# Softmax weights left unscaled until a head pair is mixed; the reciprocal sums travel through DRAM

## The chip, the core and the metric

The kernel runs on one core of a Trainium2 chip. The core has TensorE (PE in the profile, with its weight loader PEld), VectorE (DVE), ScalarE (ACT), GpSimd (POOL) and SyncE (SP), which issues most of the DMAs. The metric is the device time of one execution in microseconds (us). All arithmetic is float32; products are made in the float32r format from a high and a low part of each operand, so most data exist as two tiles, `hi` and `lo`.

## The reference

Two layers on 512 frames of 1024 channels. The first mixes by pooling, the second by attention; each ends in a gated MLP. What the change touches is the attention of the second layer, with 16 heads of 64 channels; for 512 frames its band is causal by chunks of 64 and covers all earlier chunks.

```python
q = head_rmsnorm(q.reshape(B, S, N_HEADS, HEAD_DIM), q_norm)
k = head_rmsnorm(k.reshape(B, S, N_HEADS, HEAD_DIM), k_norm)
...
    s = jnp.einsum('bqhd,bkhd->bhqk', qc, kb).astype(jnp.float32) * scale + bias[None]
    s = jnp.where(valid[None, None, None, :], s, -1e30)
    p = jax.nn.softmax(s, axis=-1).astype(vb.dtype)
    return jnp.einsum('bhqk,bkhd->bqhd', p, vb)
...
return o @ w_o
```

## The kernel before

The residual stream X is kept channel-major: 8 tiles of 128 channels by 512 frames. The attention first projects and forms the values V (`opening`), then runs a loop over 64 tiles: 16 heads, and for each head 4 tiles `t` of 128 query frames, tile `t` seeing `(t+1)*128` keys. Two heads make a pair `p`, and a pair's result is one tile O2 of 128 channels (64 of each head) by 512 frames.

One step of the loop works on several tiles at once, shifted by `LAG` = 2 and `LAGM` = 2 steps:

- `scores(h, t)`: PE makes the scores of a tile in PSUM (`sc`, L1394 and L1395). DVE adds the bias B and writes the tile `sb` with its row minimum (L1398). ACT takes the exponential and its row sum (L1400). DVE takes the reciprocal of the sum (L1401), and ACT multiplies the tile by it (L1402). At a head's first tile two DMAs on SP load its bias from DRAM (L1389).
- `turn(h, t)`, two steps later: PE transposes the tile in blocks of 128x128 (`tp`, L1410), and ACT and DVE split it into high and low parts (`pt0h`, `pt0l` for even heads, `pt1h`, `pt1l` for odd ones; by the helper `split`, L102 and L103).
- `mix(h)`, two steps after a head's last `turn`: PE multiplies V with the transposed tiles (`oo`, L1422); the products with V's high and low part lie in different halves of the partitions, so ACT copies one (`ob`, L1427) and DVE adds the other into the pair's O2 (`o`, L1428).
- `channel_major(p, i)`: PE transposes queries and keys of the next pair (`zt`), POOL and SP's DMAs bring them into the forms that `scores` reads (`z`, `zh`).

PE's order is written by hand (`manual_schedule`); between the steps `fill` puts PE work in proportion: the last part of the second projection, the third and fourth, and from step 35.5 on the output projection `outputs` (tiles `wo`). This needs O2 split into high and low parts (`two<-o` in the profile, L102 and L103), which is written once a pair is done and its room is free. The output projection takes pairs 0 to 3, then 4 and 5; pairs 6 and 7 (`wo_6`) come after the loop. X is added by DVE (L1348).

On the other engines, and on SP, the order in the loop is made by a scheduler that simulates the program when it is built. Each engine runs its own rows strictly in that order, and a row that waits holds all rows behind it. POOL splits the weights of the projections (L103), and up to pair 5 also both parts of the output weights (L100 and L103).

Of the kernel before, what the change touches and what calls it, by code (L numbers as in the profile page):

```python
# [17 lines left out]
F32 = mybir.dt.float32  # L18
F32R = mybir.dt.float32r
AF = mybir.ActivationFunctionType  # L20
# [3 lines left out]
P = 128  # L24
S = 512
# [5 lines left out]
HD = 64  # L31
NPAIR = H // 2
TT = S // P
# [39 lines left out]
def trunk(ctx: ExitStack, tc: tile.TileContext, xt, xT, cols, band, edge, poolw, gv, wout, wqk, wv, wo, rel, out):  # L73
    nc = tc.nc
# [3 lines left out]
    tmp = ctx.enter_context(tc.tile_pool(name="tmp", bufs=1))  # L78
    dram = ctx.enter_context(tc.tile_pool(name="dram", bufs=1, space=bass.MemoryType.DRAM))
# [9 lines left out]
    def psum(tag, name, bufs=2):  # L89
        return ps.tile([P, S], F32, name=name, tag=tag, bufs=bufs)  # L90
# [3 lines left out]
    def g_tile(name):  # L94
        return tmp.tile([P, S], F32, name=name, tag="g", bufs=6)
# [45 lines left out]
    def small(name, n, tag="nw"):  # L141
        return tmp.tile([P, n], F32, name=name, tag=f"{tag}{n}", bufs=4)
# [213 lines left out]
    ones = consts.tile([P, 1], F32, name="ones")  # L356
    gq = consts.tile([P, 2], F32, name="gq")
    rdram = dram.tile([H, RLEN], F32, name="rdram")
    ET = mybir.EngineType
    with tc.tile_pool(name="start", bufs=1) as sp, tc.manual_schedule(engines={ET.PE, ET.DVE, ET.Activation, ET.Pool, ET.SP}):  # L360
        first, second, acc0 = mixer(sp)

    def ffn(l, first, pool, acc, summed=None, upool=None, hook=None):
# [56 lines left out]
        def early():  # L420
# [6 lines left out]
            for at, (f, k, i) in enumerate(units):  # L427
# [13 lines left out]
                if at == (19, 14)[l]:  # L441

                    order = tc.manual_schedule(engines={ET.DVE, ET.Activation}) if l == 0 else nullcontext()
                    order.__enter__()
# [388 lines left out]
        def tour():  # L833
# [8 lines left out]
            def place(f, k):  # L842

                for word in PLACES[k].split():
                    x, name = word.split(".")
                    step = steps_of(f + "qofn".index(x) - 2).get(name)
                    if step:
                        step()

            for f in range(KIND.index("s"), NF + 2):  # L850
# [10 lines left out]
                for k in range(7):  # L861
                    if (f, k) == (ORDERED, 0):
                        order.enter_context(tc.manual_schedule(engines={ET.DVE, ET.Activation, ET.SP}))
                    place(f, k)
# [50 lines left out]
    def attention(rest, hook, hidden_slots):  # L915
        XS = set2
        O2, V, Z, QK, SM = {}, {}, {}, {}, {}
# [463 lines left out]
        def scores(h, t):  # L1381

            p, e = divmod(h, 2)
            q, k, kl = QK[p, 0][e], QK[p, 1][e], KL[p % 2][e]
            if t == 0:

                base = rdram[h, :]
                for r, n in ((0, S - HD), (HD, S)):
                    nc.sync.dma_start(BT[h % 2][r:r + HD, S - n:], bass.AP(tensor=base.tensor, offset=base.offset + HD, ap=[[1, HD], [1, n]]))  # L1389
            n = (t + 1) * P  # L1390
            nw = max(n, 256)

            sc = psum("S", f"sc{h}_{t}", 4)
            nc.tensor.matmul(sc[:, :nw], q[:, t * P:n], k[:, :nw], start=True, stop=False)  # L1394
            nc.tensor.matmul(sc[:, :nw], q[:, t * P:n], kl[:, :nw], start=False, stop=True)  # L1395
            SM[h, t] = s_ = heads.tile([P, n], F32, name=f"sb{h}_{t}", tag=f"sb{t}")
            mx = tmp.tile([P, 3], F32, name=f"mx{h}_{t}", tag="mx", bufs=4)
            nc.vector.tensor_tensor_reduce(out=s_[:, :n], in0=sc[:, :n], in1=BT[h % 2][:, :n][:, ::-1], scale=1.0,  # L1398
                                           scalar=3e38, op0=OP.add, op1=OP.min, accum_out=mx[:, 0:1])
            nc.scalar.activation(s_[:, :n], s_[:, :n], AF.Exp, scale=-1.0, bias=mx[:, 0:1], accum_out=mx[:, 1:2])  # L1400
            nc.vector.reciprocal(mx[:, 2:3], mx[:, 1:2])  # L1401
            nc.scalar.activation(s_[:, :n], s_[:, :n], AF.Copy, scale=mx[:, 2:3])  # L1402

        def turn(h, t):

# [7 lines left out]
        def mix(h):  # L1413

            p, e = divmod(h, 2)
            hs = slice(e * HD, (e + 1) * HD)
            oo = psum("S", f"oo{h}", 4)
            if p not in O2:
                O2[p] = heads.tile([P, S], F32, name=f"o2_{p}", tag="o2", bufs=4)
            for c in range(2):  # L1420
                for j in range(TT):
                    nc.tensor.matmul(oo[:, j * P:], V[j, h // 4][:, h % 4].rearrange("p a d -> p (a d)"),  # L1422
                                     PT[e][c][:, 4 * j:3 * j + TT].rearrange("p t q -> p (t q)"),
                                     start=j == 0 and c == 0, stop=j == TT - 1 and c == 1)
            ob = g_tile(f"ob{h}")
            other = slice(HD - e * HD, 2 * HD - e * HD)
            nc.scalar.activation(ob[hs], oo[other], AF.Copy)  # L1427
            nc.vector.tensor_add(O2[p][hs], oo[hs], ob[hs])  # L1428

        r2, late = small("r2", TT), []  # L1430
        closing = ExitStack()
        with tc.tile_pool(name="pre", bufs=1, reuse_waits="tile") as pre:
            with tc.manual_schedule(engines={ET.PE, ET.DVE, ET.Activation, ET.SP}):
                rcol, second = opening(pre)
        heads = closing.enter_context(tc.tile_pool(name="bh", bufs=1, reuse_waits="tile"))
# [9 lines left out]
        with tc.manual_schedule(engines={mybir.EngineType.PE}):  # L1445
# [17 lines left out]
            for i in range(nb + LAG + LAGM):  # L1463
                steps = []
                if i < nb:
                    steps.append(lambda: scores(*tiles_[i]))
                if i % 8 in CM and i // 8 + 1 < NPAIR:
                    steps.append(lambda: channel_major(i // 8 + 1, CM.index(i % 8)))
                j = i - LAG
                if 0 <= j < nb:  # L1470
                    steps.append(lambda: turn(*tiles_[j]))
                j2 = j - LAGM
                if 0 <= j2 < nb and j2 % TT == TT - 1:
                    steps.append(lambda: mix(tiles_[j2][0]))
                for x, step in enumerate(steps):
                    step()
                    if late and x < 2:
                        late.pop(0)()
                    fill(i + (x + 1) / len(steps))

                while 8 * kept + 7 <= j2 and (cur == 3 or cur == 2 and done >= 24 * (kept // 2 + 1)):
                    split(O2[kept], XS[kept], XS[KD + kept])
                    kept += 1
# [41 lines left out]
    with tc.tile_pool(name="ba", bufs=1, reuse_waits="tile") as big:  # L1525
        rest = attention(rest, hook, hidden_slots)
# [55 lines left out]
```

## Time and profile before

| | |
|---|---|
| runs, median (lowest to highest) | 966.68 us (966.43 to 966.88) |
| profiled execution, its own time | 969.2 us |
| its span, first to last instruction | 967.4 us |
| head loop in it | about 440 to 605 us |
| ACT busy / DVE busy, whole span | 594.0 us / 849.5 us |
| DMA, mean over the span | 107 GB/s |

A page names an engine, the line of the kernel, the operation and its tiles (`out<-in`); a helper's line, such as L103, stands for many callers, so tiles tell them apart. PE's matmuls are pipelined, so "busy" is not the same as working at full pace; the time from one start to the next shows the pace. A row's idle time in brackets is that of the engine just before it, with what ended it.

### The profile page before, as it was taken

Reading aid. Unit: us, or ns where it says so; the run is one execution under the profiler, and the core shown is the slowest. Engines: PE = TensorE matmul, PEld = TensorE weight load, DVE = VectorE, ACT = ScalarE, POOL = GpSimd, SP = SyncE. Lnnn points to the kernel's source line nnn. Section 1 sums busy time; section 2 is a strip of 40 time slices with the busy share of each in tenths; the row PEclk is TensorE's granted clock in tenths of the full one; section 3 lists DMA queues with packets and bytes.
Section 4 is the critical chain, followed back from the end, with each engine's and each line's share of the span. In section 5 each row is a group of like instructions: output and inputs, shape, how many; then the busy total and the mean of one; then the engine's idle time right before and its main releaser. Section 6 shows DMA issues by size and latency. Waiting matters only on the chain.

```text
span 967.4 us, 13737 instructions
## 1 busy us (share of the span) xinstructions
PE 956.3 (99%) x4958; PEld 810.0 (84%) x4958; DVE 849.5 (88%) x1522; ACT 594.0 (61%) x1023; POOL 91.2 (9%) x81
## 2 busy tenths in 40 slices
PE   8999999999999999999999999999999999999998
PEld 7788988888888888888888777888988888888886
DVE  8999999999899859895786887999999999989953
ACT  7665554655555457466898888656565565456531
POOL 2300000000000000043525441000000000000000
PEclk9999999999999999999999999999999999999999
DMA  9222332332323317024433341332333233332323
GB/s 343 73 97 71 115 108 81 120 120 80 114 79 120 102 48 292 21 66 133 132 113 97 88 117 55 100 109 80 94 115 108 84 120 111 102 104 79 114 79 111
DMA packets 38996, 103.87 MB, mean 107 GB/s; under 512 B 4464, under 2 KB 7936, under 8 KB 38928
## 3 DMA queue, kind: packets, MB, share of 16 engines
q1 hardware_dynamic: 38864, 102.95, 33.0%
q8 instruction: 39, 0.64, 0.3%
q14 instruction: 29, 0.24, 0.1%
q0 software_dynamic: 32, 0.04, 0.0%
q10 hardware_dynamic: 32, 0.00, 0.0%
HBM read 96.65 MB, written 2.14 MB: 102 GB/s over the span
## 4 chain that ended last, share of the span: by engine, by line
PE 87%; DVE 8%; ACT 2%; DMA 1%; issue 1%; SPq 0%; POOL 0%; DVEq 0%; ACTq 0%; POOLq 0%
PE st_m L593 10%; PE out L124 8%; PE out L125 8%; PE out L123 8%; PE st_m L595 5%; PE st_t L593 5%; PE gv L124 4%; PE gv L125 4%; PE gv L123 4%; PE qk L123 3%; PE qk L124 3%; PE qk L125 3%; PE st_t L595 3%; PE st_b L593 3%; PE tp L1410 1%; PE st_b L595 1%
## 5 line engine op out<-in xcount | busy, mean ns | idle before, releaser
L124 PE MATMUL out<-one,ow_h 128*128 128x512 f32 x224 | 88.1, 393 | 0.0
L123 PE MATMUL out<-one,ow_h 128*128 128x512 f32 x224 | 88.0, 393 | 0.0
L125 PE MATMUL out<-one,ow_l 128*128 128x512 f32 x224 | 87.9, 393 | 0.0
L829 DVE TENSOR_TENSOR X<-out,X 128x512 f32<-128x512 f32 (+1 forms) x65 | 44.3, 683 | 45.9 <-PE out L125 45.6
L593 PE MATMUL st_m<-two,g_h 128*128 128x512 f32 x240 | 75.1, 394 | 0.1
L593 PE MATMUL st_m<-h,g_h 128*128 128x512 f32 x240 | 74.1, 390 | 0.0
L392 ACT ACTIVATE ow_h<-wo_r 128x768 fp32r<-128x768 f32 (+1 forms) x56 | 44.4, 794 | 43.4 <-PE out L124 39.8
L407 DVE SCALAR_TENSOR_TENSOR c<-a,col,c 128x511 f32<-128x511 f32 (+1 forms) x76 | 56.8, 749 | 0.0
L593 PEld LDWEIGHTS st_m<-h,g_h 128*128 128x128 f32 x240 | 45.1, 188 | 10.3
L595 PEld LDWEIGHTS st_m<-two,g_l 128*128 128x128 f32 x240 | 45.0, 188 | 9.6
L593 PEld LDWEIGHTS st_m<-two,g_h 128*128 128x128 f32 x240 | 44.0, 188 | 10.4 <-ACT w L602 0.8
L393 DVE TENSOR_TENSOR ow_l<-wo_r,ow_h 128x768 fp32r<-128x768 f32 (+1 forms) x56 | 50.4, 899 | 2.3 <-ACT ow_h L392 2.3
L602 ACT ACTIVATE w<-st_m 128x512 f32<-128x512 f32 x30 | 18.0, 598 | 55.2 <-PE st_m L595 55.2
L595 PE MATMUL st_m<-h,g_l 128*128 128x256 f32 x240 | 48.3, 283 | 0.0
L595 PE MATMUL st_m<-two,g_l 128*128 128x256 f32 x240 | 47.6, 280 | 0.0
L124 PEld LDWEIGHTS out<-one,ow_h 128*128 128x128 f32 x224 | 42.4, 189 | 5.7 <-DVE one L418 0.3
L125 PEld LDWEIGHTS out<-one,ow_l 128*128 128x128 f32 x224 | 42.4, 189 | 5.5
L123 PEld LDWEIGHTS out<-one,ow_h 128*128 128x128 f32 x224 | 42.4, 189 | 5.4
L1398 DVE CUSTOM_DVE_ANT_0 sb<-sc,B 128x128 f32<-128x128 f32 (+1 forms) x64 | 31.1, 486 | 17.9 <-PE sc L1395 13.3
L404 ACT ACTIVATE c<-a,col 128x512 f32<-128x512 f32 x38 | 30.7, 813 | 23.8 <-DVE a L751 22.2
L392 ACT ACTIVATE g_h<-gv_r 128x1024 fp32r<-128x1024 f32 x32 | 33.7, 1055 | 13.5 <-DMA gv_r<-gv 12.9
L1400 ACT ACTIVATE sb<-sb,mx 128x128 f32<-128x128 f32 (+1 forms) x64 | 35.7, 558 | 9.8 <-DVE mx L1398 9.2
(459 smaller groups left out, 3035.7 us busy)
## 6 DMA issues: line engine op xcount, KB each, us to landing
gv_r<-gv SPq DMA_DIRECT2D x86, 512.0 KB, 3.9
wo_r<-wout SPq DMA_DIRECT2D x32, 384.0 KB, 3.1
wo_r<-wout SPq DMA_DIRECT2D x32, 320.0 KB, 2.9
wqk_r<-wqk SPq DMA_DIRECT2D x12, 512.0 KB, 3.5
b<-wv SPq DMA_DIRECT2D x8, 512.0 KB, 6.7
wo_r<-wo SPq DMA_DIRECT2D x8, 512.0 KB, 3.6
xt<-xt SPq DMA_DIRECT2D x4, 512.0 KB, 5.2
X<-xT SPq DMA_DIRECT2D x8, 256.0 KB, 7.5
```

The costliest lines, as they stand in the source:

```text
L123: yield nc.tensor.matmul(o, sh, mh, start=first, stop=False, **how)
L124: yield nc.tensor.matmul(o, sh, ml, start=False, stop=False, **how)
L125: yield nc.tensor.matmul(o, sl, mh, start=False, stop=last, **how)
L392: nc.scalar.activation(hi[:, :n], raw[:, :n], AF.Copy)
L393: return hi, lo, lambda: nc.vector.tensor_sub(lo[:, :n], raw[:, :n], hi[:, :n].bitcast(F32))
L404: nc.scalar.activation(c, a, AF.Identity, scale=cw[2], bias=cw[3])
L407: nc.vector.scalar_tensor_tensor(c[:, j:], a[:, :S - j], cw[2 - j], c[:, j:], op0=OP.mult, op1=OP.add)
L593: nc.tensor.matmul(o, hi[:, c], B[i, name], start=first and i == 0, stop=False, **how)
L595: nc.tensor.matmul(o[:, 0], lo[:, c], B[i, name][:, 0], start=False, stop=i == 3, **how)
L829: nc.vector.tensor_add(X[d][:, fs], o[:, fs], X[d][:, fs])
L1398: nc.vector.tensor_tensor_reduce(out=s_[:, :n], in0=sc[:, :n], in1=BT[h % 2][:, :n][:, ::-1], scale=1.0, scalar=3e38, op0=OP.add, op1=OP.m ...
L1400: nc.scalar.activation(s_[:, :n], s_[:, :n], AF.Exp, scale=-1.0, bias=mx[:, 0:1], accum_out=mx[:, 1:2])
```

## The change

The tile of exponentials is not multiplied by the reciprocal of its sum any more. It is transposed, split and mixed as it is. The 8 sums of a pair (2 heads by 4 tiles, 128 query frames each) are collected in one tile `sums`, 128 partitions by 8. After the last exponential of a pair one DVE reciprocal gives `rr`; a DMA on SP writes it to DRAM turned around (`rinv`, 8 rows of 128 floats), and two more read it back, 512 floats of a head spread over that head's 64 partitions (`rb`). When the pair is mixed, one multiplication of O2 by `rb` puts the scale in: on POOL for pairs 0 to 6, on DVE for the last. `rb` has one buffer; O2 has three instead of four.

```diff
+    rinv = dram.tile([NPAIR, 2 * TT, P], F32, name="rinv")
...
-            mx = tmp.tile([P, 3], F32, name=f"mx{h}_{t}", tag="mx", bufs=4)
+            mx = tmp.tile([P, 1], F32, name=f"mx{h}_{t}", tag="mx", bufs=4)
+            if e == 0 and t == 0:
+                sums[p] = tmp.tile([P, 2 * TT], F32, name=f"sums{p}", tag="sums", bufs=2)
+            c = e * TT + t
...
-            nc.scalar.activation(s_[:, :n], s_[:, :n], AF.Exp, scale=-1.0, bias=mx[:, 0:1], accum_out=mx[:, 1:2])
-            nc.vector.reciprocal(mx[:, 2:3], mx[:, 1:2])
-            nc.scalar.activation(s_[:, :n], s_[:, :n], AF.Copy, scale=mx[:, 2:3])
+            nc.scalar.activation(s_[:, :n], s_[:, :n], AF.Exp, scale=-1.0, bias=mx[:, 0:1], accum_out=sums[p][:, c:c + 1])
+            if c == 2 * TT - 1:
+                rr = tmp.tile([P, 2 * TT], F32, name=f"rr{p}", tag="rr", bufs=2)
+                nc.vector.reciprocal(rr, sums.pop(p))
+                nc.sync.dma_start(rinv[p].rearrange("c q -> q c"), rr)
+                RB[p] = heads.tile([P, S], F32, name=f"rb{p}", tag="rb")
+                for b in range(2):
+                    nc.sync.dma_start(RB[p][b * HD:(b + 1) * HD], rinv[p, b * TT:(b + 1) * TT, :].rearrange("c q -> (c q)")[None].to_broadcast([HD, S]))
...
-                O2[p] = heads.tile([P, S], F32, name=f"o2_{p}", tag="o2", bufs=4)
+                O2[p] = heads.tile([P, S], F32, name=f"o2_{p}", tag="o2", bufs=3)
...
+            if e:
+                (nc.gpsimd if p < NPAIR - 1 else nc.vector).tensor_mul(O2[p], O2[p], RB.pop(p))
```

The scheduler puts the rows of the engines in a new order. Three places matter. In the rows a number after a name tells one use of a tile from the next; line numbers after the change are up to 11 higher.

The first is on ACT in heads 14 and 15, the last two: `sb_1` is head 15's tile with `t` = 1, `two_99<-o_6` the high part of pair 6. Before:

```order
L1402 ACTIVATE sb_0_6161<-sb_0_6161,mx_0_6162 128x128
L1400 ACTIVATE sb_1_6180,mx_1_6181<-sb_1_6180,mx_1_6181 128x256
L102 ACTIVATE pt0h<-tp_3_6190 128x4x128
L1402 ACTIVATE sb_1_6180<-sb_1_6180,mx_1_6181 128x256
L102 ACTIVATE pt1h<-tp_0_6210 128x128
L1400 ACTIVATE sb_2_6202,mx_2_6203<-sb_2_6202,mx_2_6203 128x384
L102 ACTIVATE pt1h<-tp_1_6228 128x2x128
```

and after the change:

```order
L1404 ACTIVATE sb_1_6116,sums_6007<-sb_1_6116,mx_1_6117 128x256
L102 ACTIVATE pt0h<-tp_3_6124 128x4x128
L102 ACTIVATE two_99<-o_6_5987 128x512
L102 ACTIVATE pt1h<-tp_0_6142 128x128
L1404 ACTIVATE sb_2_6136,sums_6007<-sb_2_6136,mx_2_6137 128x384
L102 ACTIVATE pt1h<-tp_1_6164 128x2x128
```

The copies L1402 are gone; pair 6's high part, which stood just ahead of the first row shown, now stands behind the fourth transposed tile of head 14.

The second is POOL's end: the weights of the output projection for pairs 4 and 5 (`wo_4`, two loads) are split there. Before:

```order
L1375 CAST z_0_5899<-zh_0_5898 64x512
L1375 CAST z_1_5931<-zh_1_5930 64x512
L100 CAST wo_4_h<-wo_4_r 128x1024
L103 TENSOR_TENSOR wo_4_l<-wo_4_r,wo_4_h 128x1024
L100 CAST wo_4_h<-wo_4_r 128x1024
L103 TENSOR_TENSOR wo_4_l<-wo_4_r,wo_4_h 128x1024
```

and after:

```order
L1376 CAST z_0_5846<-zh_0_5845 64x512
L1376 CAST z_1_5876<-zh_1_5875 64x512
L1439 TENSOR_TENSOR o_5_5772<-o_5_5772,rb_5761 128x512
L100 CAST wo_4_h<-wo_4_r 128x1024
L103 TENSOR_TENSOR wo_4_l<-wo_4_r,wo_4_h 128x1024
L100 CAST wo_4_h<-wo_4_r 128x1024
L1439 TENSOR_TENSOR o_6_5987<-o_6_5987,rb_5975 128x512
L103 TENSOR_TENSOR wo_4_l<-wo_4_r,wo_4_h 128x1024
```

The products stand in POOL's queue between the weight splits; that of pair 6 has the last low part behind it, and that of pair 3 (not shown) the second low part of `wo_0`.

The third is the end of the loop on SP and PE. SP after the change (before, the same rows stand there without `rinv` and `rb`, and the two loads of `wo_6` side by side):

```order
L1390 DMA B_4308<-rdram 64x512
L1408 DMA rinv<-rr_5972 128x8x1
L117 DMA gv_0_1_r<-gv 128x1024
L1411 DMA rb_5975<-rinv 64x512 x2
L117 DMA wo_6_r<-wo 128x4x256
L1408 DMA rinv<-rr_6157 128x8x1
L1411 DMA rb_6160<-rinv 64x512 x2
L117 DMA wo_6_r<-wo 128x4x256
L375 DMA wo_0_0_r<-wout 128x640
```

PE's first products with pairs 6 and 7, before (all into the first output tile, three with pair 6 and three with pair 7, whose high parts are the two halves of `two_99`):

```order
L123 MATMUL wo_6_6351<-two_99,wo_6_h 128x512
L124 MATMUL wo_6_6351<-two_103,wo_6_h 128x512
L125 MATMUL wo_6_6351<-two_99,wo_6_l 128x512
L123 MATMUL wo_6_6351<-two_99,wo_6_h 128x512
L124 MATMUL wo_6_6351<-two_103,wo_6_h 128x512
L125 MATMUL wo_6_6351<-two_99,wo_6_l 128x512
```

and after:

```order
L123 MATMUL wo_6_6288<-two_99,wo_6_h 128x512
L124 MATMUL wo_6_6288<-two_103,wo_6_h 128x512
L125 MATMUL wo_6_6288<-two_99,wo_6_l 128x512
L123 MATMUL wo_6_6296<-two_99,wo_6_h 128x512
L124 MATMUL wo_6_6296<-two_103,wo_6_h 128x512
L125 MATMUL wo_6_6296<-two_99,wo_6_l 128x512
L123 MATMUL wo_6_6288<-two_99,wo_6_h 128x512
```

The reads of `rb` stand behind the write of `rinv` on the same queue, and the second load of `wo_6` behind the reads of the last pair. On PE the products of pair 6 with a second output tile now stand ahead of the first product with pair 7. DVE's last rows change with it: the product of pair 7 stands between two additions of X, and its split one addition later.

More of the change, by code (lines that the diff above doesn't have):

```diff
@@ L1428, in mix @@
             nc.vector.tensor_add(O2[p][hs], oo[hs], ob[hs])
-        r2, late = small("r2", TT), []
+            if e:
+                (nc.gpsimd if p < NPAIR - 1 else nc.vector).tensor_mul(O2[p], O2[p], RB.pop(p))
+        r2, late, sums, RB = small("r2", TT), [], {}, {}
         closing = ExitStack()
```

## The prediction

> **What bounds the kernel now.** I read the page first, then busy time by stretch, then the waits of TensorE inside the attention, and last the timeline at its longest wait.
>
> ```profile
> PE 956.3 (99%) x4958; PEld 810.0 (84%) x4958; DVE 849.5 (88%) x1522; ACT 594.0 (61%) x1023; POOL 91.2 (9%) x81
> 440.00:540.00 100.00, 100.00 (x541) 84.28 (x540) 69.01 (x211) 84.78 (x205) 43.23 (x33) 1.00 0.37 112
> 540.00:605.00 65.00, 60.82 (x340) 49.33 (x338) 54.49 (x156) 53.79 (x137) 22.53 (x17) 1.00 0.29 84
> 605.00:965.00 360.00, 358.66 (x1854) 306.23 (x1852) 319.03 (x507) 191.59 (x279) 0.00 (x0) 1.00 0.31 101
> ```
>
> TensorE (PE) is busy for 956.3 of 967.4 us, so only what it waits can be won. The three stretches are the head loop while it has projections to fill in (440 to 540), the head loop while it fills in the output projection (540 to 605), and what follows. In the first PE is busy 100.00 of 100; in the last 358.66 of 360. In the middle it is 60.82 of 65: 4.2 us of idle time, and that is where ScalarE (ACT, 53.79) and VectorE (DVE, 54.49) are both busy over 80%. Freeing ACT in the first stretch gives nothing.
>
> ```profile
> PE tp L1410 <- ACT sb L1402: 3.2, 5, 1.7
> PE oo L1422 <- DVE pt1l L103: 0.5, 1, 0.5
> PE sc L1394 <- DMA zh<-zh: 0.3, 1, 0.3
> PEld tp L1410 <- ACT sb L1402: 6.1, 8, 2.1
> ```
>
> Of that idle time 3.2 us is PE waiting to transpose a tile whose scaling copy (L1402) is not done. The weight loader (PEld), which waits first, lost 6.1 us to it. The true loss lies between, and the longest wait shows where.
>
> ```profile
> 576.64 0.51 ACT L1400 ACTIVATE sb<-sb,mx 128x256 f32<-128x256 f32 x1
> 577.28 2.38 POOL L103 TENSOR_TENSOR wo_l<-wo_r,wo_h 128x1024 fp32r<-128x1024 f32 x1
> 577.29 2.92 DVE L103 TENSOR_TENSOR two<-o,two 128x512 fp32r<-128x512 f32 x1
> 578.84 0.40 PE L123 MATMUL wo<-two,wo_h 128*128 128x512 f32 x1
> 580.13 0.15 DVE L1401 RECIPROCAL mx<-mx 128x1 f32<-128x1 f32 x1
> 580.21 0.53 DVE L1398 CUSTOM_DVE_ANT_0 sb<-sc,B 128x384 f32<-128x384 f32 x1
> 580.32 0.51 ACT L1402 ACTIVATE sb<-sb,mx 128x256 f32<-128x256 f32 x1 [2.15 <-DVE mx L1401]
> 580.78 0.62 ACT L1400 ACTIVATE sb<-sb,mx 128x384 f32<-128x384 f32 x1
> 580.88 0.20 PEld L1410 LDWEIGHTS tp<-ident,sb 128*128 128x128 f32 x2 [2.07 <-ACT sb L1402]
> 580.89 0.43 PE L1410 MATMUL tp<-ident,sb 128*128 128x128 f32 x2 [1.65 <-ACT sb L1402]
> ...
> 608.87 0.39 PE L123 MATMUL wo<-two,wo_h 128*128 128x512 f32 x1
> 609.10 0.39 PE L124 MATMUL wo<-two,wo_h 128*128 128x512 f32 x1
> ```
>
> The last two rows give PE's pace on 512 columns: 0.23 us from start to start. From 578.84 to 580.89 it is 2.05, so 1.82 is lost, where PE's idle column says 1.65 and PEld's 2.07: 40% of the way up. Over all such waits that makes 3.2 + 0.4 x 2.9 = 4.4 us, and I count **4.5** with the small ones on other ACT rows.
>
> These rows also show the cause. The exponential of the awaited tile began at 576.64 and took 0.51. Then DVE sat in the low part of a split (L103) for 2.92 us while GpSimd (POOL) ran 2.38 us over the same time; only then came the reciprocal (580.13), the copy (580.32) and the transpose. Without reciprocal and copy this tile is ready at about 577.2, and the whole 1.82 goes.
>
> **The change, part by part.**
>
> ```profile
> L1400 ACT ACTIVATE sb<-sb,mx 128x128 f32<-128x128 f32 (+1 forms) x64 | 35.7, 558 | 9.8 <-DVE mx L1398 9.2
> L1402 ACT ACTIVATE sb<-sb,mx 128x128 f32<-128x128 f32 (+1 forms) x64 | 35.5, 556 | 3.8 <-DVE mx L1401 3.0
> L1400 ACT ACTIVATION_READ_ACCUMULATOR sb<-sb,mx 128x1 f32 x64 | 12.1, 190 | 0.0
> L1401 DVE RECIPROCAL mx<-mx 128x1 f32<-128x1 f32 x64 | 10.1, 158 | 7.7 <-ACT sb L1400 7.5
> L1321 POOL TENSOR_TENSOR z<-z,qk_y 128x512 f32<-128x512 f32 x12 | 12.6, 1082 | 14.6 <-DVE qk_y L1319 14.6
> L103 DVE TENSOR_TENSOR two<-o,two 128x512 fp32r<-128x512 f32 x8 | 8.6, 1071 | 0.1
> ```
>
> *Removed.* 64 copies, 35.5 us of ACT; 56 of 64 reciprocals (56 x 0.158 = 8.8 us of DVE; the 8 that are left have 8 columns, one per head and tile, and feed nothing that a transpose waits for). All of it lies beside PE, so its worth is the 4.5 us of waits above. ACT and DVE then have room, so that no new wait on the exponential takes their place: the next tile's exponential began at 580.78, behind the late DVE row of 580.21, and was wanted only some 2 us later.
>
> *Costed at nothing.* The accumulator reads stay (190 ns each, now into a column of sums). O2 has three buffers instead of four: a pair's buffer is free once its split is done, and the pair that wants it comes three pairs later. In the first stretch, where PE never waits, the same products and DMAs cost only what they delay on POOL and SP, and both have gaps there.
>
> *Added on POOL.* Seven multiplications 128x512, like L1321, 1.08 each, 7.6 us; POOL is busy 43.23 of 100 and 22.53 of 65, so there is room. But they read two operands in SBUF, and so does DVE's split two<-o (eight, mean 1071 ns; one of them is the 2.92 above). The order puts POOL's next weight split right behind the product for pairs 3 and 6, just when DVE gets to two<-o.
>
> ```profile
> 590.23 2.40 POOL L103 TENSOR_TENSOR wo_l<-wo_r,wo_h 128x1024 fp32r<-128x1024 f32 x1
> 591.90 0.69 DVE L1428 TENSOR_TENSOR o<-oo,ob 64x512 f32<-64x512 f32 x1
> ```
>
> For pair 6: now POOL's split is over at 592.6, when DVE's sum (591.90) is. After the change POOL waits for that sum, multiplies to 593.7 and splits until 596.1, across DVE's two<-o. I expect two or three waits of DVE of 1 to 2 us, of which little reaches PE, since the tile's way to the transpose has lost two steps. Bounds: nothing, and 2 x 1.82, as the one of before cost; near the lower end, **0.5**.
>
> [...]
>
> What stands behind the new waits: on ACT two<-o now waits for POOL's product instead of DVE's sum, and behind it stand the next tile's transposed copy (pt1h) and exponential, so a late product reaches PE within a tile. On DVE the product of pair 7 waits for the DMA, and behind it stand the additions that free the banks of the output projection.
>
> *Added on SyncE (SP).* Per pair one DMA of 128x8 single floats to DRAM and two that read 64 rows of 2 KB back, each behind the one before. While SP waits for the first to land, everything behind it on SP waits too.
>
> ```profile
> B<-rdram SPq DMA_DIRECT2D x16, 128.0 KB, 3.1
> rdram<-rs POOLq DMA_DIRECT2D x1, 39.9 KB, 2.4
> edg<-edge ACTq DMA_DIRECT2D x1, 4.0 KB, 2.8
> q1 hardware_dynamic: 38864, 102.95, 33.0%
> ...
> 546.86 1.10 SPq L1389 DMA_DIRECT2D B<-rdram  x2
> 554.91 0.48 SPq L1378 DMA_DIRECT2D z<-zl  x1
> 582.18 2.00 SPq L1389 DMA_DIRECT2D B<-rdram  x2
> 584.28 0.53 SPq L117 DMA_DIRECT2D gv_r<-gv  x1
> ```
>
> Reading back is like B<-rdram: 3.1 to land, 0.55 to issue each (1.10 for two at 546.86). The writing DMA, call its time to land L, has no like here. Below, the write rdram<-rs: 2.4; the same 4 KB in edg<-edge: 2.8. Above, 1024 packets at the mean of q1, 0.330 x 16 x 967.4 / 38864 = 0.131 us each, 64 on each engine, 8.4 + 2.4 = 10.8. I take **4**, near the row with the same bytes. Queue time costs nothing at 4: after the bias loads of a pair's last tile SP issues nothing for 7 us (547.96 to 554.91), and write and reads take 0.5 + 4 + 1.1.
>
> [...]
>
> *When L decides.* Pair 6: the write can go at 584.2 (behind the two B of 582.18), the second read at 584.2 + L + 0.55, landed at 587.9 + L; POOL wants it at 592.6 and ACT has some 1 us more. Pair 7:
>
> ```profile
> 597.49 0.72 ACT L1400 ACTIVATE sb<-sb,mx 128x512 f32<-128x512 f32 x1 [0.48 <-DVE mx L1398]
> 604.37 0.69 DVE L1428 TENSOR_TENSOR o<-oo,ob 64x512 f32<-64x512 f32 x1 [0.42 <-ACT ob L1427]
> 605.10 0.63 ACT L102 ACTIVATE two<-o 128x512 fp32r<-128x512 f32 x1 [0.76 <-DVE o L1428]
> ```
>
> The last exponential ends at 597.49 + 0.72, its accumulator is read by 598.4, reciprocal 598.6; landed at 602.25 + L; product 0.69, ACT's high part 0.63: ready at 603.6 + L. PE's first product with pairs 6 and 7 is at 608.87; six products instead of three now stand ahead of the first that needs pair 7, so it is wanted at 610.2, less about 1 us that PE gains after that exponential: 609.2. Both pairs put the limit near **L = 5.6**. At 4 there is no wait; with the longer path (the product itself, DVE's X additions behind it) I leave **0.5**.
>
> **Sum**: 969.2 (the profiled execution's own time; its span is 967.4) - 4.5 + 0.5 + 0.5 = 965.7. The median of the runs is 2.5 below that execution, so **963.2**.
>
> **Rivals.** (a) *All waits of PE go*, also those on oo, sc and the loader's others, nothing comes back: 966.7 - 6 = 960.7. For: ACT and DVE both get lighter. Against: the waits on oo and sc name DVE and a DMA, not the copy. 10%. (b) *Given back*: L between 5.6 and 8, or DVE held by POOL at pairs 3, 5 and 6 at the full price. 3 to 4.5 us are returned, which gives 965.2 to 966.7; 22%. For: the 2.92 row. That the copy was never the cause (PE would wait for the exponential instead) has the same result, and the row of 576.64 speaks against it. (c) *Slower: the element-wise write is slow.* At L = 10.8 pair 7 comes 5.2 us late; DVE, in order, holds the X additions behind the product and ACT the gate weights; pairs 4 to 6 come 4 to 5 us late for POOL, ACT and PE behind it, of which I count 3. 966.7 - 4.5 + 5.2 + 3 = 970.4; it is slower than before from about L = 8.5 on. 12%.
>
> **How the numbers follow.** The forecast has 56% (961.5 to 964.8). The range reaches from 960.8 (case a) to 967.8: the upper end takes in (b) and leaves out (c). A measurement of this kernel can tell about 0.2%, 1.9 us, from no change. Faster: the forecast and (a), with little of (b) and less a bit of the forecast's upper end: 0.64. Same: most of (b), 0.24. Slower: (c), 0.12.
>
> **What would show it.** Right: in the stretch that was 540 to 605, PE's waits for ACT on tp fall from 3.2 to under 0.5 and no new row takes their place; that stretch is 3 to 4 us shorter and the 360 us behind it are unchanged; rinv lands in 3 to 5 us. Wrong: PE or PEld waiting on rb, on o or on two in the last 20 us of the head loop; POOL's products waiting on DMA rb; DVE two<-o at 2 to 3 us three times, with PE idle behind each; a landing of rinv above 5.6.

## The result, and the profile after

The changed kernel takes **990.3 us** (median of 4 runs, 989.8 to 993.6) against 966.8 for the kernel before on the same chip: a ratio of 1.025, 95% interval 1.0228 to 1.0273. That is 23.5 us slower; the prediction was 963.2, with 967.8 as its upper end. The profiled execution took 990.3 itself, so its trace stands for the median.

Busy time and the stretches come first. The stretches hold the same work as 440 to 540, 540 to 605 and what follows before; the last has been cut at 642, where the output projection is over. Columns are the stretch, its length, busy time and instructions of PE, PEld, DVE, ACT and POOL, then the granted clock of TensorE, DMA share and GB/s.

```profile
PE 965.1 (98%) x4958; PEld 813.9 (82%) x4958; DVE 846.1 (86%) x1467; ACT 565.2 (57%) x959; POOL 100.9 (10%) x88
442.00:542.00 100.00, 98.68 (x534) 83.04 (x533) 63.93 (x174) 68.29 (x166) 46.79 (x35) 1.00 0.44 108
542.00:616.50 74.50, 63.99 (x341) 52.37 (x340) 54.34 (x132) 40.92 (x107) 28.73 (x22) 0.95 0.49 98
616.50:642.00 25.50, 20.28 (x81) 16.10 (x80) 16.56 (x25) 13.75 (x20) 0.00 (x0) 0.87 0.33 105
642.00:986.00 344.00, 342.78 (x1776) 290.91 (x1774) 303.21 (x484) 177.53 (x260) 0.00 (x0) 1.00 0.30 98
```

ACT has become lighter, as said (565.2 us against 594.0). But PE now has gaps in all three of the first stretches: 1.3 us in the one that had none, 10.5 us in the one that had 4.2, and 5.2 us behind it, where there were none before. Its clock is granted at 0.95 and 0.87 there, where it was 1.00. The waits from 430 to 642 say on what. (Each line has the engine, tile and line that waited and what it waited for, then the sum in us, how many times, and the longest.)

```profile
PE wo L123 <- DVE X L1349: 5.2, 1, 5.2
PE oo L1431 <- DVE pt0l L103: 3.8, 1, 3.8
PE sc L1395 <- DMA zh<-zh: 3.6, 2, 2.3
PE tp L1419 <- DVE pt1l L103: 2.6, 1, 2.6
PE tp L1419 <- ACT pt1h L102: 1.2, 1, 1.2
POOL o L1439 <- DMA rb<-rinv: 17.8, 5, 7.2
ACT two L102 <- POOL o L1439: 9.4, 4, 4.1
DVE o L1439 <- DMA rb<-rinv: 7.8, 1, 7.8
```

The row `tp <- ACT sb`, 3.2 us before, is gone. In its place stand waits that all lead to one DMA: POOL and DVE wait 25.6 us for `rb`, ACT waits for POOL's product, PE for what ACT and DVE do behind that, and for `zh`, whose moves stand behind it on SP. SP's view of the DMAs (count, size, median us to landing) and SP's timeline at the last two pairs name it:

```profile
rinv<-rr SPq DMA_DIRECT2D x8, 4.0 KB, 9.7
rb<-rinv SPq DMA_DIRECT2D x16, 128.0 KB, 3.5
z<-zl SPq DMA_DIRECT2D x8, 128.0 KB, 4.5
...
590.49 0.54 SPq L1408 DMA_DIRECT2D rinv<-rr  x1
600.56 1.09 SPq L1411 DMA_DIRECT2D rb<-rinv  x2
610.83 0.37 SPq L1408 DMA_DIRECT2D rinv<-rr  x1
621.54 1.09 SPq L1411 DMA_DIRECT2D rb<-rinv  x2
```

The write `rinv` takes 9.7 us to land, where I had put 4. The reads of pairs 6 and 7 go out 10.1 and 10.7 us after the writes. What else is issued in the meantime lands late too (`z<-zl` 4.5, before 2.3). For pair 7 the write is issued at 610.83, because the loop is late by then, and PE stands until 626.59:

```profile
626.59 0.79 PE L123 MATMUL wo<-two,wo_h 128*128 128x512 f32 x1 [5.22 <-DVE X L1349]
627.18 0.63 PE L124 MATMUL wo<-two,wo_h 128*128 128x512 f32 x1
627.61 0.63 PE L125 MATMUL wo<-two,wo_l 128*128 128x512 f32 x1
...
620.00:630.00 10.00, 4.78 (x15) 3.53 (x14) 4.67 (x7) 3.28 (x4) 0.00 (x0) 0.69 0.36 111
```

Behind that wait the starts are 0.43 us apart (627.18, 627.61), not the 0.23 of before. The granted clock falls to 0.5 in three pieces, 13.7 us together: two begin about 1 us behind PE's idle times of 3.8 and 2.6 us, the third 2.4 us into the longest, which is 5.2. The matmuls that PE starts in these pieces come 4.9 us later than at the usual distance. So about a fifth of the loss is the clock, not the wait. The pieces last 3.413, 3.413 and 6.827 us. How much idle time brings one about is not shown: the idle time before the second piece is 2.6 us, one of 2.3 (to 570.14) has no piece behind it, and in the run e13_low below a piece of 3.413 follows two idle times of 1.0 and 1.3.

### The profile page after: what moved, and what is told of

It is laid out like the page before. It is cut to its first block, busy times and chain, and to the rows that moved or that the text cites. A ratio compares the mean times of both kernels' runs of the same rounds, so it can differ in the third digit from the quotient of the medians.

```text
span 988.5 us, 13704 instructions
## 1 busy us (share of the span) xinstructions
PE 965.1 (98%) x4958; PEld 813.9 (82%) x4958; DVE 846.1 (86%) x1467; ACT 565.2 (57%) x959; POOL 100.9 (10%) x88
## 3 DMA queue, kind: packets, MB, share of 16 engines
q1 hardware_dynamic: 48464, 105.08, 34.6%
## 4 chain that ended last, share of the span: by engine, by line
PE 83%; DVE 9%; DMA 5%; issue 1%; ACT 1%; POOL 0%; SPq 0%; DVEq 0%; POOLq 0%; ACTq 0%
PE st_m L594 10%; PE out L125 8%; PE out L124 8%; PE out L123 8%; PE st_m L596 5%; PE st_t L594 5%; PE gv L124 4%; PE gv L125 4%; PE gv L123 4%; DMA rinv<-rr 3%; PE qk L125 3%; PE qk L123 3%; PE qk L124 3%; PE st_t L596 3%; PE st_b L594 3%
## 5 line engine op out<-in xcount | busy, mean ns | idle before, releaser
L594 PEld LDWEIGHTS st_m<-h,g_h 128*128 128x128 f32 x240 | 45.1, 188 | 10.2
L594 PEld LDWEIGHTS st_m<-two,g_h 128*128 128x128 f32 x240 | 44.0, 188 | 10.9 <-ACT v L603 0.9
L1402 DVE CUSTOM_DVE_ANT_0 sb<-sc,B 128x128 f32<-128x128 f32 (+1 forms) x64 | 31.1, 486 | 24.1 <-PE sc L1396 23.5
L393 ACT ACTIVATE g_h<-sa 128x1024 fp32r<-128x1024 f32 x32 | 33.8, 1056 | 12.1 <-DVE sa L639 7.3
```

Source lines behind the costliest of these rows:

```text
L393: nc.scalar.activation(hi[:, :n], raw[:, :n], AF.Copy)
L594: nc.tensor.matmul(o, hi[:, c], B[i, name], start=first and i == 0, stop=False, **how)
```

## The experiments

Theory 1: the loss is the element-wise write. It has four forms: 1a, SP stands behind it, and moves and loads of the next pair come late; 1b, the product comes late; 1c and 1d, its packets hold up their own queue, or all queues. Theory 2: POOL's products and DVE's splits shut each other out. Theory 3: the scheduler's new order on DVE and ACT. Two more came up on the way: 4, that the new small tiles move other tiles, and 5, that part of the 4.5 us to be won belonged to one execution only.

"PE's loss" is worked out from the starts of PE's matmuls between 430 and 660 us: each distance from start to start, less the median for its shape, summed. It was 8.5 us in the profile that I predicted from. A median of the 512-column shape that is 1 ns off moves it by some 0.8 us.

| run | median us | ratio to before, 95% | write lands in, us | PE's loss, us |
|---|---|---|---|---|
| after | 990.3 | 1.0250 (1.0228 to 1.0273) | 9.7 | 25.2 |
| e1_rows | 969.2 | 1.0023 (1.0013 to 1.0032) | 2.3 | 4.3 |
| e2_poolq | 994.6 | 1.0269 (1.0249 to 1.0288) | 10.0 | 31.0 |
| e3_noprod | 982.8 | 1.0156 (1.0138 to 1.0173) | 10.1 | 16.5 |
| e4_dvet | 969.5 | 1.0025 (1.0016 to 1.0034) | - | 3.9 |
| e5_line | 987.6 | 1.0215 (1.0198 to 1.0231) | 9.8 | 25.6 |
| e6_shift | 969.6 | 1.0026 (1.0014 to 1.0037) | none | 4.4 |
| e7_turned | 967.0 | 1.0003 (0.9994 to 1.0012) | - | 6.7 |
| e8_traffic | 988.3 | 1.0221 (1.0207 to 1.0235) | 10.1, 10.0 | 27.9 |
| e9_before | 966.7 | 0.9994 (0.9984 to 1.0004) | none | 5.2 |
| e10_twos | 968.6 | 1.0010 (1.0001 to 1.0019) | 4.1 | 6.7 |
| e11_actq | 984.6 | 1.0173 (1.0155 to 1.0190) | 10.2, 8.0 | 23.8 |
| e12_dve | 968.1 | 1.0007 (0.9998 to 1.0016) | - | 6.4 |
| e13_low | 972.5 | 1.0047 (1.0034 to 1.0060) | - | 11.0 |
| e14_blow | 972.1 | 1.0045 (1.0033 to 1.0058) | none | 9.6 |
| e15_dlow | 971.2 | 1.0042 (1.0028 to 1.0055) | - | 8.0 |

A dash marks writes for which the profile gives no landing time.

### The write, and who pays for it

**e1_rows**: the same bytes, written as they lie.

```diff
-                nc.sync.dma_start(rinv[p].rearrange("c q -> q c"), rr)
+                nc.sync.dma_start(rinv[p].rearrange("c q -> (c q)").rearrange("(q c) -> q c", c=2 * TT), rr)
```

> The kernel after, but the reciprocals go to DRAM as they lie in SBUF (128 rows of 32 bytes in place of 1024 single floats); the two reads, the products and the order of every compute engine stay. The sums land on the wrong queries, so the scaling is left out in effect. Theory 1 (the element-wise write is the cause): it lands in 2.5 to 4 us like the other 4 KB row (2.8), SP is free again early, and the time falls to 962 to 967 us, below the kernel before. Theory 2 (POOL's products and DVE's splits shut each other out) and theory 3 (the new order on DVE and ACT): both stay as they are, so the time stays at 983 to 991.

The write lands in 2.3 us and the time falls by 21 us. Every engine's order is that of the changed kernel, but for one pair's reads on SP, which move ahead of a weight load, so theories 2 and 3 are out for the bulk of the loss. A rest stays: 969.2 is 2 us above the range of theory 1, and above the kernel before. The second row is the longest wait that PE has left in 535 to 650; it comes up again below.

```profile
rinv<-rr SPq DMA_DIRECT2D x8, 4.0 KB, 2.3
PE tp L1419 <- ACT pt1h L102: 1.1, 1, 1.1
```

**e2_poolq** and **e3_noprod** take the two ways apart in which the write could cost: the first issues the reads from POOL's queue, the second leaves out the product.

```diff
-                    nc.sync.dma_start(RB[p][b * HD:(b + 1) * HD], ...
+                    nc.gpsimd.dma_start(RB[p][b * HD:(b + 1) * HD], ...
...
-                (nc.gpsimd if p < NPAIR - 1 else nc.vector).tensor_mul(O2[p], O2[p], RB.pop(p))
+                RB.pop(p)
```

> The kernel after, but the two reads of a pair are issued from POOL's queue, so that SP never stands behind the write (which stays element by element, 9.7 us). Theory 1a (the loss is SP's: moves of the next pair's queries and the bias loads come late): the waits of PE for zh (1.5 and 2.5 us) and what follows from them go, 966 to 974. Theory 1b (the loss is the late product: ACT and DVE stand behind it): those waits of PE go too, but the long ones on oo, tp and wo (4.1, 2.8 and 5.4 us, and the half clock behind them) stay, 980 to 988. Theories 2 and 3: 985 to 991.

> The kernel after, with the write and the reads as they are and no product (the scaling by 1/sum is left out). SP still stands behind each write for some 9 us. Theory 1a: the time stays at 980 to 988. Theory 1b: only the two waits for zh stay, 966 to 972. Theory 2 gives the same 966 to 972 here and is told apart from 1b by the run with rows.

e2_poolq missed all its ranges. POOL's queue now stands behind the write, and with it the weight splits, and PE waits for `zh` as long as ever (3.6 us):

```profile
POOL rb L1411 <- DMA rinv<-rr: 72.1, 8, 16.0
PE wo L125 <- POOL wo_l L103: 10.6, 3, 5.2
PE sc L1395 <- DMA zh<-zh: 3.6, 2, 1.9
```

This does not speak against 1a, for e2_poolq has only moved the standing: SP's moves of `zh` also wait for POOL's casts `z<-zh`, and these now stand behind the reads. The rows at the longest such wait of PE in the changed kernel, and at one in e2_poolq:

```profile
552.12 0.37 SPq L1408 DMA_DIRECT2D rinv<-rr  x1
567.78 0.54 SPq L1379 DMA_DIRECT2D zh<-zh  x1
570.14 0.36 PE L1395 MATMUL sc<-zh,zh 128*128 128x256 f32 x1 [2.29 <-DMA zh<-zh]
```

```profile
567.50 1.09 POOL L1411 DMA_DIRECT2D rb<-rinv  x2 [7.69 <-DMA rinv<-rr]
569.71 1.18 POOL L1376 CAST z<-zh 64x512 fp32r<-64x512 f32 x2
571.57 0.54 SPq L1379 DMA_DIRECT2D zh<-zh  x1
```

In the changed kernel POOL's cast is done at 559.2, but the move goes out at 567.78, behind the write and the reads; it then lands in 2.3 us, as before the change. In e1_rows the same move goes out at 558.83. From 430 to 642 SP stands 70.8 us for the write, in e1_rows 12.8. So SP's standing does make `zh` late here, as 1a says.

In e3_noprod nobody computes with `rb`; 7.5 us of the 21 go, 13.6 stay (982.8 against 969.2), which lies in 1a's range. Yet about half of the 13.6 is still a wait for `rb`: by the profile ACT's split of the gate weights, which does not read it, waits 8.0 us for its last landing (until 617.63), PE behind that loses 4.9, and 2.3 more at the half clock. So both ways are real, and how the loss divides between them isn't shown. **e8_traffic** and **e11_actq** ask for the mechanism: the slow write goes to a DRAM tile that nobody reads (`rslow`), ahead of a fast one in rows, which the reads then use; first on SP's queue, then on ACT's.

```diff
+                nc.sync.dma_start(rslow[p].rearrange("c q -> q c"), rr)
-                nc.sync.dma_start(rinv[p].rearrange("c q -> q c"), rr)
+                nc.sync.dma_start(rinv[p].rearrange("c q -> (c q)").rearrange("(q c) -> q c", c=2 * TT), rr)
```

> The kernel e5_line with two writes per pair: first the element-wise one into a DRAM tile that nobody reads, then the reciprocals in rows as in e1_rows, which the reads then use (the scaling is left out in effect). Nobody waits for the slow write any more, but its 1024 packets still go through SP's queue, ahead of the other write. Theory 1 in the form that the wait of SP and of the product for one landing is the loss: rows land in 2.5 us, 966 to 968. Theory 1 in the form that the packets hold up the queue for whatever is issued behind them: rows and what follows land some 7 us later than in e1_rows, and the time stays at 980 to 988.

> The kernel e8_traffic with the slow write, which nobody reads, on ACT's queue in place of SP's (the scaling is left out in effect). Theory 1c (the packets hold up only what is behind them in their own queue): rows land in 2.5 us and the time falls to 966 to 969. Theory 1d (they occupy the 16 engines for every queue): rows land in some 5 to 10 us and the time stays at 975 to 988.

```profile
rslow<-rr SPq DMA_DIRECT2D x8, 4.0 KB, 10.1
rinv<-rr SPq DMA_DIRECT2D x8, 4.0 KB, 10.0
```

```profile
rslow<-rr ACTq DMA_DIRECT2D x8, 4.0 KB, 10.2
rinv<-rr SPq DMA_DIRECT2D x8, 4.0 KB, 8.0
```

The first pair of rows is e8_traffic, the second e11_actq. The write in rows, 2.3 us by itself, takes 10.0 behind the slow one on the same queue and 8.0 with the slow one on another engine's queue. The time stays at 988.3 and 984.6. In e11_actq, where both writes are issued within 0.6 us of each other, the eight landings range from 1.5 to 12.1; behind two that got through in 1.5 the reads took 11.1 to 11.4 in place of 3. So the 1024 packets hold up what is issued beside and behind them, on SP's queue or on ACT's, as 1d has it; that they do so by occupying the 16 engines is not shown. What this costs by itself the two runs do not say, for SP still stands 71.9 and 50.4 us in them, behind the held-up write. **e10_twos** measures the price: half as many packets, on the base of e5_line (below).

```diff
-                nc.sync.dma_start(rinv[p].rearrange("c q -> q c"), rr)
+                nc.sync.dma_start(rinv[p].rearrange("c q -> (c q)").rearrange("(k q x) -> q k x", q=P, x=2), rr.rearrange("q (k x) -> q k x", x=2))
```

> The kernel e5_line with the reciprocals written two at a time, 512 packets of 8 bytes (in another order, so that the scaling is left out in effect). Theory 1 with a price per packet: 128 packets landed in 2.3 and 1024 in 9.7, that is 8.3 ns each, so 512 land in 5.5 us; PE's long waits are nearly gone and the time is 967 to 973. If the landing depends on the bytes or on the pattern and not on the packets: 2.5 or 9.7 us, and 967 or 987.

512 packets land in 4.1 us, 1024 in 9.7, 128 in 2.3: it is the number of packets (or their size) and not the bytes in all, though not in proportion (4.7 ns each from 128 to 512, 10.9 from there to 1024, as differences of the medians). At 4.1, my own value for L, the time is 968.6. The waits for `rb` are gone but for one, 2.4 us of DVE at the last pair; it comes up again below.

### The tiles that moved

e1_rows and **e4_dvet**, which turns the reciprocals around on VectorE and writes 32 rows of 128 bytes, agree in being 2 to 2.5 us above before, although PE's loss in them is the smallest of all runs.

```diff
+                nc.vector.transpose(rt, rr)
-                nc.sync.dma_start(rinv[p].rearrange("c q -> q c"), rr)
+                for g in range(4):
+                    nc.sync.dma_start(rinv[p, :, g * 32:(g + 1) * 32], rt[g * 32:g * 32 + 2 * TT])
```

> A full kernel: VectorE turns the reciprocals around in 32x32 blocks (one more small row on DVE per pair), and four DMAs of 8 rows of 128 bytes write them, so DRAM gets 32 packets a pair and not 1024. Theory 1: each lands in some 2.5 us, the last about 4 us after the first is issued; 962 to 967, faster than before by up to 0.5%. Theories 2 and 3: 983 to 991.

The mean distance of PE's 512-column matmuls in the last 335 us (starts less than 0.3 us apart) is 231.6 ns in e1_rows and 231.3 in e4_dvet, and 229.6 in the kernel before. What they share with the changed kernel is `sums` and `rr`: 4 small tiles of 32 bytes a partition in the pool `tmp`, which move every pool that is opened later by 128 bytes (448 in e4_dvet, whose tiles are wider). Before, all of these but the two on the right-hand side started at multiples of 512, which the filler of the constants (`LINE`) sees to. **e5_line** puts the four tiles into that filler; **e6_shift** adds 128 unused bytes to the kernel before.

```diff
-    consts.tile([P, (LINE - CONST) // 4], F32, name="fill0")
+    consts.tile([P, (LINE - CONST) // 4 - 8 * TT], F32, name="fill0")
+    sums2, rr2 = ([consts.tile([P, 2 * TT], F32, name=f"{x}_{b}") for b in range(2)] for x in ("sums", "rr"))
...
+        nc.gpsimd.memset(tmp.tile([P, 32], F32, name="shift"), 0.0)
```

> The kernel after, order and all, except that the 128 bytes a partition of the new small tiles (two of sums, two of reciprocals) lie in the filler of the constants and not behind the other small tiles, so that every later pool starts at a multiple of 512 bytes again, as before the change. Theory 4 (matmuls read slower from tiles that do not start on such a line): the mean pitch of 512-column matmuls in the last 335 us goes back from 231.7 to about 229.9 ns and early on from 231.4 to 230.8, and the time falls by about 3 us, to 986.5 to 988.5. Without theory 4 the time stays at 990 to 992.

> The kernel before with one unused tile of 128 bytes a partition behind the small tiles (and one small memset of it), which moves every later pool by 128 bytes, as the change does. Theory 4: 2 to 3.5 us slower than before, 969 to 970.5, with the pitch of 512-column matmuls at 231.7 ns in the last 335 us. Without theory 4: as before, 966.5 to 967.5.

Both came out as theory 4 has it: 987.6 (2.7 less than the changed kernel, though the intervals of the two ratios just touch), and 969.6 (2.6 more than before, ratio 1.0026, which is clear of 1). The distance defined above is back at 229.6 ns in e5_line and is 231.6 in e6_shift. The same 80 matmuls, first of the kernel before (e9_before, below), then of e6_shift, from PE's timeline:

```profile
933.79 0.39 PE L123 MATMUL out<-one,ow_h 128*128 128x512 f32 x1
951.92 0.39 PE L125 MATMUL out<-one,ow_l 128*128 128x512 f32 x1
```

```profile
936.22 0.40 PE L123 MATMUL out<-one,ow_h 128*128 128x512 f32 x1
954.89 0.40 PE L125 MATMUL out<-one,ow_l 128*128 128x512 f32 x1
```

18.13 us against 18.67: 226.6 and 233.4 ns each, with no wait in either.

**e7_turned** mends both: e4_dvet with its small tiles in the filler.

> A full kernel: the reciprocals turned around on VectorE and written as 32 rows of 128 bytes, as in the run e4_dvet, and the small tiles in the filler of the constants, as in e5_line. Theories 1 and 4 together: 969.5 less 3, so 965.5 to 967.0. If what is left of the loss has another cause: 968.5 to 970.

967.0, at the upper end: the same as before within 0.1%. The two faults account for the loss (20.5 us from e5_line to e7_turned, 2.7 from the changed kernel to e5_line, together 23.2 of 23.5), and the gain that the change was to bring isn't there.

### Where the gain is

**e9_before** is the kernel before, profiled once more.

> The kernel before, unchanged: a second profile of it. Theory 5 (of the 4.5 us that were to be won, the 1.8 us at 580.89 and the 0.5 at 565.17 belong to that one execution, where VectorE's split two<-o had to wait for GpSimd; its own time was 2.5 above the median): here PE waits on tp for ACT's copy about 1.6 us and not 3.2, two<-o beside POOL's split takes 0.7 us, and the own time lies within 1 us of the median. Without theory 5: 3.2 us again, with the long row of 2.9 us.

This execution took 966.7. The rows that answer to those of the prediction:

```profile
PE tp L1410 <- ACT sb L1402: 1.5, 4, 0.8
PEld tp L1410 <- ACT sb L1402: 4.3, 8, 1.3
L103 DVE TENSOR_TENSOR two<-o,two 128x512 fp32r<-128x512 f32 x8 | 6.3, 791 | 0.1
```

The wait on the copy is 1.5 us and not 3.2, the split two<-o takes 791 ns and not 1071: the 2.92 us row is not there, nor PE's 1.82 behind it. e6_shift shows the same (4.4 us of PE's loss). So 1.8 of the 2.5 us by which the execution that I predicted from lay above the median are this. The other 0.5 that theory 5 names, at 565.17, was a wait for the DMA of `zh`, 12 us ahead of this split; it is gone in e9_before too.

Of the rest, some 2.7 us, the waits on the copy do go in e7_turned, but two others stand there. Its profiled execution took 968.3, 1.3 above its median; e10_twos, profiled at its median, has the same two. The first, in its timeline:

```profile
542.05 1.29 POOL L1442 TENSOR_TENSOR o<-o,rb 128x512 f32<-128x512 f32 x1 [2.27 <-DVE o L1440]
543.30 2.40 POOL L103 TENSOR_TENSOR wo_l<-wo_r,wo_h 128x1024 fp32r<-128x1024 f32 x1
543.49 2.27 DVE L1319 TENSOR_TENSOR qk_a<-qk_s,r 128x32 f32<-128x32 f32 x1
...
546.72 0.41 PE L1422 MATMUL tp<-ident,sb 128*128 128x128 f32 x2 [1.14 <-ACT pt1h L102]
```

POOL's product (542.05) pushes its weight split to 543.30, where in e9_before it began at 539.90. DVE's small row at 543.49, beside that split, takes 2.27 us, in e9_before 0.17; ACT's `pt1h` and PE's transpose come behind it, and PE loses 1.3 us. (In e9_before PE lost 1.0 at this place, to ACT's copy.) In the changed kernel the same row takes 2.40. This is rival (b) of the prediction, on a row that I had not named. The second wait is the last pair's way through DRAM:

```profile
605.19 0.69 DVE L1442 TENSOR_TENSOR o<-o,rb 128x512 f32<-128x512 f32 x1 [2.33 <-DMA rb<-rinv]
612.82 1.22 DVE L103 TENSOR_TENSOR wo_l<-wo_r,wo_h 128x1024 fp32r<-128x1024 f32 x1
614.09 0.50 PE L125 MATMUL wo<-two,wo_l 128*128 128x512 f32 x1 [1.34 <-DVE wo_l L103]
```

DVE's product waits 2.33 us for `rb`. Behind it ACT's high parts of pair 7, of the gate weights and of the second load of `wo_6` come about 3 us later than in e9_before, DVE's `wo_l` 2 us later, and PE loses 1.5. In e1_rows, whose last write landed in 1.4 us, the product does not wait and PE loses 0.25 there. PE's loss in e1_rows is 4.3 us, against 5.2 in e9_before: with a quick write some 1 us of the gain is left, too little to tell from none. A quick write in rows with the layout mended was not run.

**e12_dve** puts all products on DVE:

```diff
-                (nc.gpsimd if p < NPAIR - 1 else nc.vector).tensor_mul(O2[p], O2[p], RB.pop(p))
+                nc.vector.tensor_mul(O2[p], O2[p], RB.pop(p))
```

> The kernel e7_turned with all eight products on VectorE, 0.69 us each in place of 1.3 on GpSimd. Theory 2 (the product on POOL costs something beside DVE's splits, and makes the next weight split late, 1.5 us of PE at 614): 964 to 966, faster than before. Otherwise 966.5 to 968.

The wait at 546 is gone, and 1.8 us of PE appear at 580, where two<-o lies beside a split of POOL again (2.67 us). The time is 968.1, which is not the gain that theory 2 forecast. The last three runs move POOL's six low parts of the output weights to DVE: in e7_turned, in the kernel before, and in e12_dve.

```diff
-                w[d] = load_split(..., D, f"wo{d}_{p0}", eng=eng, eng_hi=eng)
+                w[d] = load_split(..., D, f"wo{d}_{p0}", eng=None, eng_hi=eng)
```

> The kernel e7_turned with the low parts of the output weights on VectorE (1.2 us each, six more) and not on GpSimd (2.4). Theory 5b (the copies' worth is taken back where VectorE waits for GpSimd's splits): PE's waits of 1.3 us at 546 and 1.5 at 614 go, 964 to 965.5. Theory 5c (the copies were worth nothing): 966.5 to 968, or slower where VectorE becomes too full.

> The kernel before with the same move of the six low parts to VectorE. Theory 5b: VectorE and ACT are as full as ever, the waits of tp for ACT's copy (1.5 to 3.2 us) stay or grow, 966.5 to 969, 2 us or more above e13_low. Theory 5c: the same time as e13_low within 0.7 us.

> The kernel e12_dve (all products on VectorE) with the same move: GpSimd has next to no work with two SBUF operands left in 540 to 605. Theory 5b: no row of VectorE above 1.3 us there, the wait of 1.76 us at 580 goes, 964 to 966. Theory 5c: 967 to 969.

All three are slower, 971.2 to 972.5; that DVE is too full to take the splits is my estimate, from its busy time (55.1 of the 65 us from 540 to 605 in e7_turned) and the 1.22 us that a low part takes it there. 5b's forecasts failed: of its waits only that at 580 went (e15_dlow), those at 546 and 614 stayed. 5c's came true: e14_blow and e13_low, which differ in the change alone (as e7_turned has it), are as long as each other within 0.7 us. That DVE's long rows beside POOL's splits take gain back is shown in two places (2.27 us at 543 in e7_turned, 2.67 at 577 in e12_dve); that the gain is to be had without it isn't shown, since taking it away cost more. The first row is e14_blow, the second e13_low:

```profile
PE tp L1410 <- ACT sb L1402: 5.1, 6, 2.0
```

```profile
PE wo L125 <- DVE wo_l L103: 1.3, 1, 1.3
```

The copy makes PE wait 5.1 us in e14_blow. In e13_low there is none to wait for, and PE waits for DVE's row minimum (1.1 at 545), at `zt` (twice 0.9 us at 554), for X (1.2 at 614) and for the weights (1.5 at 617) instead, and then runs 3.4 us at half its clock. My reading, which no run shows by itself: in these 80 us PE waits for DVE, of which the change takes 3.4 us in 849.5, and, at the last pair, for the DMA; not for ACT, of which it takes 29. Whether some other order would turn the removed copies into time stays open; none of the 15 runs was measurably faster than the kernel before.

## Why the prediction was wrong, step by step

- **The element-wise write (L = 4).** This is the step that failed most: "near the row with the same bytes". It measured 9.7. Bytes were the wrong likeness; the upper bound of 10.8, from the packets, was 1.1 from the truth, partly by luck: it priced packets of 4 bytes at the mean of packets of 2.6 KB. Its count of one packet to a float held: the changed kernel's queue has 8 x 896 more packets than that of e1_rows (48464 against 41296).
- **"Queue time costs nothing at 4."** At 4.1 nearly true (e10_twos, 968.6), but for the last pair: the limit of 5.6 followed only PE's first product with it, and what stands behind its product on ACT and DVE, put at 0.5, cost 1.5. At 9.7 SP stands behind every write and the packets hold up a write of 2.3 us to 10.0 on SP's queue (e8_traffic) and, from ACT's, to 8.0 (e11_actq), so pairs 4 to 6 lose as well, and the first stretch, which I called free, loses 1.3 us.
- **Rival (c)** had the slow write, near its right size, and the place (pairs 4 to 6, then 7), but not the held-up queues. Its time was off, 970.4 against 987.6 with the layout mended: the delays add up from pair to pair, the last write starts late itself, and in the changed kernel 4.9 us are the halved clock.
- **The 4.5 us of the copies.** The row did go, as said. But 1.8 of the 4.5 belonged to one execution, and the sum then took off 2.5 more for the median: largely the same microseconds twice. What was left, some 2.7 us, came back as a wait on `pt1h` behind DVE (1.3 us) and on the last weights (1.5, in e7_turned). That "no new row takes their place" was wrong.
- **POOL's products (0.5).** They take 1.29 us each, not 1.08, and push a split of POOL over a row of DVE; I gave 0.5 to all of it, and PE lost 1.3 at that one place (e7_turned), where the row took 2.27 us beside POOL's split of 2.40, and 0.17 in e9_before. Of the pairs that rival (b) names, pair 6 has a slow split on DVE in the changed kernel (2.16 us at 606.68), pair 5 none (0.83 at 587.03).
- **Not seen at all**: the new tiles move the large ones off their multiples of 512 bytes, 2.6 us (e6_shift). "The 360 us behind it are unchanged" was wrong for this reason.
- **Right**: the waits on the copy went; the read back lands like the bias (said 3.1; 3.0 in e1_rows, 3.5 in the changed kernel); no wait that the profile names is for O2's third buffer.

## What to carry to other kernels

Price a DMA by its packets, not its bytes (here the same 4 KB landed in 2.3, 4.1 and 9.7 us as 128, 512 and 1024 packets); ask what is issued beside and behind it on any queue (here a write of 2.3 us took 8.0 and 10.0), and what stands behind the first row that needs it. Where a sum starts from one profiled execution that lies off the median, find the rows that make the difference before subtracting anything from it. And look where new small tiles lie: they can move every large one (here 2.6 us, e6_shift).

## What the runs showed of the hardware

- 1024 packets of 4 bytes to DRAM land in 9.7 us (the changed kernel), 512 of 8 bytes in 4.1 (e10_twos), 128 of 32 bytes in 2.3 (e1_rows), the same 4 KB each time; issued on ACT's queue, the first delay a write of 128 packets that SP issues at the same time from 2.3 to 8.0 (e11_actq; medians; 1.5 to 12.1).
- In one stretch of 80, PE's matmuls of 512 columns run at 226.6 ns where the large tiles start at multiples of 512 bytes in SBUF (e9_before) and at 233.4 where they start 128 bytes behind one (e6_shift; 229.6 and 231.6 over the last 335 us; 2.6 us of the kernel). Why is not shown.
- At three idle times of 2.6 to 5.2 us in the changed kernel TensorE's granted clock was halved for 3.4 to 6.8 us; after one of 2.3 (570.14) it was not.
- Which of two splits that DVE and POOL start within 0.03 us of each other is the long one differed between two executions of one program: where POOL's began at 577.28 and DVE's at 577.29, POOL's took 2.38 and DVE's 2.92 us; where DVE's began at 576.72 and POOL's at 576.75 (e9_before), it took 0.68 and POOL's 2.92. PE lost 1.8 us in the first.
